# The second block's mixer: last gate projection emitted behind all else, recurrent heads two rounds later, small casts behind the gate products

## The chip, the cores and the metric

The kernel runs on one core of a Trainium2 chip. The metric is the device time of one execution in microseconds, lower is better. Engines are named as the profile names them: PE (TensorE, matmuls), PEld (its weight loads), DVE (VectorE), ACT (ScalarE), POOL (GpSimd), SP (SyncE, which here issues the loads of weights).

## The reference

A sequence of 256 tokens of 1024 features goes through two layers of a first block and then through one layer of a second. The change lies in the second block's mixer. There `proj = x @ w_in` is split into eight parts:

```python
q_a, k_a, v_a, f_a, q_r, f_r, i_r, g_r = jnp.split(proj, SPLIT_POINTS, axis=-1)
o_a = _fox_attention(heads(q_a, 8), heads(k_a, 8), heads(v_a, 8), logf_a)
o_a = _rms_norm_heads(o_a, fox_norm_g)
o_r = _hgrn2_chunked(heads(silu(q_r), 4), heads(k_r, 4), heads(i_r, 4), heads(logf_r, 4))
o_r = _rms_norm_heads(o_r, hgrn_norm_g) * silu(g_r)
mix = concatenate([o_a, o_r], axis=-1) @ w_o
x = _layer_norm(DEEPNORM_ALPHA * x + mix, ln_mix_g, ln_mix_b)
```

The attention has 8 heads of 64 features, causal, with a decay per head (`f_a`) added to the scores. The recurrent part has 4 heads of 128 features with a decay per feature (`f_r`). Both are normalised per head; the recurrent one is multiplied by the gate `silu(g_r)`. Then come the out projection `w_o`, a layer norm, and a feed-forward part with a convolution.

## The kernel before, in words

The whole model is one program. Weights stream from memory in blocks of 128 x 1024; each is split into a high part `wh` (a cast on ACT, L317) and a low part `wl` (a subtraction on DVE, L319), and there are five buffers for such pairs. A product is made of three matmuls (high x high, low x high, high x low), so that it keeps the precision of 32-bit floats. Each engine works through its own list of instructions strictly in order; a framework fixes these lists when the program is built, from the order in which the code emits the work, the engines' estimated times and the buffers. `issue_after(i)` adds a rule for one engine: what is emitted under it comes behind instruction `i` in that engine's list.

The mixer is `mix2` (L1165 to L1494). It emits its work from four generators that a loop of ticks calls in turn (L1460 to L1479). `main` (L1266) goes through the list `ORD`, `q0, va, q1, k2, q2, k3, q3, sg`: projections with the tokens as moving operand (L344 to L346, three matmuls of 128 x 256 a step, for q and k) or with the weights as moving operand (L373 to L375, 48 matmuls of 128 x 512 in all, for `va` and for the gate `sg`). `fox` (L1385) is the attention, head by head: scores (L1394, L1395), maximum and exponential, transposes (L1416), products with the values (L1426 to L1428). After four heads it normalises the group: multiplication by the reciprocal on DVE (L1439, into the tile `mix`), squares on POOL (L1442), sums on DVE (L1443), a reciprocal root in three small steps on ACT (L499 to L501) and four on POOL (L502 to L505), multiplication on DVE (L1448). Then `mixT` transposes the result on PE (L1356), ACT writes the high part `oh` (L1357) and DVE the low part `ol` (L1358).

`hgrn_a` (L1286) makes the decay tiles E of a recurrent head: matmuls with fixed patterns (L1298, L1299), exponentials on ACT (L1300), multiplications by k and q on DVE and POOL. `hgrn_b` (L1318) makes its score tile A level by level: matmuls (L1331), each put into A through a mask by DVE (L1332), a block between the two halves of the sequence (matmul L1336, copied into A by ACT, L1337), the product with the values (L1341 to L1343), copies into `mix` on DVE (L1346) and sums of squares on ACT (`jk`, L1348).

The out projection reads 1024 features in two halves: `out_half(0)` those of the attention, `out_half(1)` those of the recurrent heads. The latter need `hgrn_end` (L1360): eight products of `mix` with the reciprocal root `rrr` and the gate `sgr` (L1365, DVE), then `mixT`. The gate's silu (L1482) and the next exponentials need different tables on ACT, so a table load stands on either side of it. `def_begin` (L1097) casts the norm's gains and biases into the tiles of the layer norm, in twelve very small DVE operations (L1108, L1109).

Before, the gate projection waits in two ways: `main` yields until `fox` has been emitted whole, and on PE it comes behind the attention's last product:

```python
while fox in live:
    yield
with self.tc.issue_after(self.last_pv.ins):
    for _ in g:
        pass
```

Of the kernel before, what the change touches and what calls it, by code (L numbers as in the profile page):

```python
# [12 lines left out]
ALU = mybir.AluOpType  # L13
AX = mybir.AxisListType

P = 128
# [198 lines left out]
class K:  # L215
# [955 lines left out]
    def mix2(self, first):  # L1171
        nc = self.nc
# [55 lines left out]
        for tt in range(2):  # L1228
# [3 lines left out]
                                           op0=ALU.mult, op1=ALU.min)  # L1232
# [3 lines left out]
                                           op0=ALU.min, op1=ALU.subtract)  # L1236
# [6 lines left out]
        def projn(dst, fn=AF.Copy):  # L1243
            ps = [self.mm_ps() for _ in range(2)]
            yield from self.proj_n(ps)
            for tt in range(2):
                nc.scalar.activation(dst[:, tt], ps[tt], fn)
# [14 lines left out]
        sg = nat("sgr")  # L1262
# [3 lines left out]
        def main():  # L1266
            for d in ORD:
                if d == "va":
                    yield from projn(va)
                    made.add(d)  # L1270
                    continue
                if d == "sg":
                    g = projn(sg)
                    while fox in live:
                        yield
                    with self.tc.issue_after(self.last_pv.ins):
                        for _ in g:
                            pass
                    continue
                dst, t, sc = (fq if d[0] == "q" else fk), int(d[1]), (0.125 if d[0] == "q" else 1.0)  # L1280
                ps = self.mm_ps()[:, :T]
                yield from self.proj_t_steps(ps)
                nc.scalar.activation(dst[:, t], ps, AF.Copy, scale=sc)
                made.add(d)
# [3 lines left out]
        def hgrn_a():  # L1288
            for h in range(4):
                while h > len(done) + 1:  # L1290
                    yield
                E = [self.slot(f"E{tt}").rearrange("p (l t) -> p l t", l=8) for tt in range(2)]
                for tt in range(2):
                    for hf in range(2):
                        ps = self.mm_ps()
                        c = slice(hf * 512, (hf + 1) * 512)
                        hs = slice(h * P, (h + 1) * P)
                        nc.tensor.matmul(ps, lh[:, tt, hs], pat[tt][:, c], start=True, stop=False)  # L1298
                        nc.tensor.matmul(ps, ll[:, tt, hs], pat[tt][:, c], start=False, stop=True)  # L1299
                        nc.scalar.activation(E[tt][:, hf * 4:hf * 4 + 4], ps.rearrange("p (l t) -> p l t", l=4), AF.Exp)  # L1300
                    yield
                k3 = kT[:, h].rearrange("p (t c) -> p t c", t=2)
                q3 = qrT[:, h].rearrange("p (t c) -> p t c", t=2)
                nc.vector.tensor_tensor(out=E[0][:, 7], in0=E[0][:, 7], in1=k3[:, 0], op=ALU.mult)
                nc.vector.tensor_tensor(out=E[1][:, 7], in0=E[1][:, 7], in1=q3[:, 1], op=ALU.mult)
                for l, B in enumerate(LEVELS):
                    for o, src in ((0, k3), (1, q3)):
                        for tt in range(2):
                            v = E[tt][:, l].rearrange("p (n s b) -> p n s b", s=2, b=B)[:, :, o]
                            s = src[:, tt].rearrange("p (n s b) -> p n s b", s=2, b=B)[:, :, o]  # L1310
                            e = nc.gpsimd if (l * 4 + o * 2 + tt) % 8 == 0 else nc.vector
                            e.tensor_tensor(out=v, in0=v, in1=s, op=ALU.mult)
                hE[h] = E
                yield

        def hgrn_b():
            for h in range(4):
                while h not in hE:  # L1318
                    yield
                E = hE.pop(h)  # L1320
                k3 = kT[:, h].rearrange("p (t c) -> p t c", t=2)
                q3 = qrT[:, h].rearrange("p (t c) -> p t c", t=2)
                A = self.ap_.tile([P, 3, P], F32, tag="A", name="A", bufs=2)
                nc.gpsimd.memset(A, 0.0)
                for l2 in range(4):
                    ps = self.six_ps().rearrange("p (a b) -> p a b", a=2)
                    for li in range(2):
                        l = 2 * l2 + li
                        for tt in range(2):
                            a, b = (E[tt][:, l], E[tt][:, l]) if l < 7 else (k3[:, tt], q3[:, tt])  # L1330
                            nc.tensor.matmul(ps[:, li, tt * P:(tt + 1) * P], a, b, start=True, stop=True)  # L1331
                        nc.vector.copy_predicated(A[:, 0:2], msk[:, l].unsqueeze(1).to_broadcast([P, 2, P]),  # L1332
                                                  ps[:, li].rearrange("p (t c) -> p t c", t=2))
                    yield
                ps = self.aux_ps()
                nc.tensor.matmul(ps[:, :P], E[0][:, 7], E[1][:, 7], start=True, stop=True)  # L1336
                nc.scalar.activation(A[:, 2], ps[:, :P], AF.Copy)  # L1337
                yield
                ps = self.aux_ps()
                hs = slice(h * P, (h + 1) * P)  # L1340
                nc.tensor.matmul(ps[:, 0:P], A[:, 0], vr[:, 0, hs], start=True, stop=True)  # L1341
                nc.tensor.matmul(ps[:, P:2 * P], A[:, 2], vr[:, 0, hs], start=True, stop=False)
                nc.tensor.matmul(ps[:, P:2 * P], A[:, 1], vr[:, 1, hs], start=False, stop=True)  # L1343
                for tt in range(2):
                    o = mixn[tt][:, 512 + h * P:512 + (h + 1) * P]
                    nc.vector.tensor_copy(o, ps[:, tt * P:(tt + 1) * P])  # L1346
                    jk = self.tmp("jk", P, 2)
                    nc.scalar.activation(jk, ps[:, tt * P:(tt + 1) * P], AF.Square,  # L1348
                                         accum_out=ssr[:, tt * 4 + h:tt * 4 + h + 1])
                done.append(h)  # L1350
                yield

        def mixT(dst, src, gain):
            ps = self.aux_ps()
            for tt in range(2):
                nc.tensor.transpose(ps[:, tt * P:(tt + 1) * P], mixn[tt][:, src * P:(src + 1) * P], self.ident)  # L1356
            self.last_mix = nc.scalar.activation(OH(dst), ps[:, :T], AF.Copy, scale=gain)  # L1357
            nc.vector.scalar_tensor_tensor(out=OL(dst), in0=ps[:, :T], scalar=gain, in1=OH(dst).bitcast(F32),  # L1358
                                           op0=ALU.mult, op1=ALU.subtract)

        def hgrn_end(rr):
            for h in range(4):
                for tt in range(2):
                    o = mixn[tt][:, 512 + h * P:512 + (h + 1) * P]
                    nc.vector.scalar_tensor_tensor(out=o, in0=o, scalar=rr[:, tt * 4 + h:tt * 4 + h + 1],  # L1365
                                                   in1=sg[:, tt, h * P:(h + 1) * P], op0=ALU.mult, op1=ALU.mult)
            for t in range(4):
                mixT(4 + t, 4 + t, self.col("hgrn_g", t))

# [87 lines left out]
        OL = lambda t: ol[t // 4][:, (t % 4) * T:(t % 4 + 1) * T]  # L1457
        fox_bias()

        gens = [[main(), 14, 0, 0], [hgrn_a(), 10, 0, 0], [hgrn_b(), 10, 0, 0], [fox(), 10, 4, 0]]  # L1460
        fox_run = gens[3]
        live = [fox]
        tick = 0
        while gens:
            for g in list(gens):
                if tick < g[2]:
                    continue
                g[3] += g[1]
                while g[3] >= 10:
                    g[3] -= 10  # L1470
                    try:
                        next(g[0])
                    except StopIteration:
                        gens.remove(g)
                        if g is fox_run:
                            live.clear()
                        break
            tick += 1
        rr = self.rsqrt(ssr, 1.0 / P, self.tmp("rrr", 8, 1))  # L1479
        with self.tc.issue_after(self.last_mix.ins):  # L1480
            for tt in range(2):
# [3 lines left out]
        for _ in self.out_half(OH, OL, 0, None, ALPHA, six=True, tiles=range(6)):  # L1485
            pass
        self.ln_begin()
        self.def_begin("ln_mix_g", "ln_mix_b")
        for _ in self.out_half(OH, OL, 1, None, None, True, tiles=range(6)):
            pass  # L1490
        for _ in self.out_half(OH, OL, 0, None, ALPHA, True, tiles=range(6, 8), kn=8):
# [179 lines left out]
```

## Time and profile before

| | us |
|---|---|
| median of 3 runs | 1342.23 |
| lowest and highest | 1341.79 and 1344.1 |
| the profiled execution | 1342.08 |
| its span | 1340.3 |
| its mean granted clock of TensorE (1 is full) | 0.995 |
| busy in the span: PE, DVE, ACT, POOL | 1315.2, 996.5, 814.2, 218.5 |

The span runs from the first to the last instruction that the profiler recorded; the execution's time has some 1.8 us more around it. The mixer's stretch of which the following speaks begins at about 1022 us of the span and ends at about 1125, with the layer norm behind it. Busy times of PE are those of pipelined matmuls that overlap: one of 512 columns is shown 0.39 us long, while such matmuls start 0.23 us apart.

### The profile page before, as it was taken

To read this page: it belongs to the slowest core of one execution; us is meant where nothing else is said; L and a number is where in the kernel's file an instruction comes from. 1 tells how busy PE (TensorE), PEld (TensorE's weight loads), DVE (VectorE), ACT (ScalarE), POOL (GpSimd) and SP (SyncE) were. 2 spreads that over 40 slices of the span, in tenths; PEclk is the share of its full clock that TensorE was granted. 3 is DMA by queue.
4 is the path that set the end of the run, shared out by engine and by line. 5 is a ranking of instruction groups with operands and counts; after the bars stand their busy time and mean duration, and the time that the engine had idled before them with its cause. 6 is when DMAs were issued, how large, how long until landed. Compare 5 with 4: busy or idle time off the path is not lost.

```text
span 1340.3 us, 22596 instructions
## 1 busy us (share of the span) xinstructions
PE 1315.2 (98%) x8250; PEld 1169.3 (87%) x8250; DVE 996.5 (74%) x1863; ACT 814.2 (61%) x1501; POOL 218.5 (16%) x252
## 2 busy tenths in 40 slices
PE   9999999899999999999999999999999999999997
PEld 8888887898888888888889888888887888899987
DVE  7877677668776768776659768777887778798754
ACT  7655546756555446555458856555567546687642
POOL 2000140021000210001334440000033122232100
PEclk9999999899999999999999999999999999999999
DMA  8555555026555556555576336555555304365561
GB/s 309 187 189 189 188 202 179 1 95 204 189 188 177 197 171 198 189 189 186 187 235 203 115 128 209 187 190 188 186 185 192 126 32 155 114 221 177 198 208 47
DMA packets 64367, 231.49 MB, mean 173 GB/s; under 512 B 7352, under 2 KB 7488, under 8 KB 64256
## 3 DMA queue, kind: packets, MB, share of 16 engines
q1 hardware_dynamic: 61632, 221.41, 49.1%
q0 software_dynamic: 2480, 8.63, 1.9%
q8 instruction: 65, 1.06, 0.3%
q14 instruction: 46, 0.38, 0.1%
q10 hardware_dynamic: 144, 0.00, 0.0%
HBM read 228.96 MB, written 1.06 MB: 172 GB/s over the span
## 4 chain that ended last, share of the span: by engine, by line
PE 92%; DVE 3%; ACT 2%; issue 2%; DMA 1%; DVEq 0%; ACTq 0%
PE mm L340 26%; PE mm L338 14%; PE sc L340 7%; PE mm L344 5%; PE mm L345 5%; PE mm L346 5%; PE mm L375 4%; PE mm L373 4%; PE mm L374 4%; PE sc L338 4%; PE mm L337 3%; PE sc L337 1%; PE aux L686 1%; PE sc L344 1%; PE sc L345 1%
## 5 line engine op out<-in xcount | busy, mean ns | idle before, releaser
L319 DVE TENSOR_TENSOR wl<-raw,wh 128x1024 fp32r<-128x1024 f32 (+1 forms) x411 | 511.8, 1246 | 240.5 <-ACT wh L317 239.1
L317 ACT ACTIVATE wh<-raw 128x1024 fp32r<-128x1024 f32 (+1 forms) x419 | 441.1, 1055 | 407.0 <-issue 209.6
L340 PE MATMUL mm<-xs,wh 128*128 128x512 f32 x826 | 294.3, 396 | 0.0
L338 PE MATMUL mm<-xs,wl 128*128 128x256 f32 x944 | 243.9, 279 | 0.1
L340 PE MATMUL mm<-h,wh 128*128 128x512 f32 x672 | 238.0, 398 | 0.0
L338 PE MATMUL mm<-h,wl 128*128 128x256 f32 x704 | 191.5, 280 | 0.0
L338 PEld LDWEIGHTS mm<-xs,wl 128*128 128x128 f32 x944 | 177.9, 188 | 10.9 <-DVE wl L319 0.4
L340 PEld LDWEIGHTS mm<-xs,wh 128*128 128x128 f32 x826 | 154.6, 188 | 31.3
L340 PEld LDWEIGHTS mm<-h,wh 128*128 128x128 f32 x672 | 126.0, 188 | 29.2
L340 PE MATMUL sc<-xs,wh 128*128 128x512 f32 x406 | 144.8, 396 | 0.0
L338 PEld LDWEIGHTS mm<-h,wl 128*128 128x128 f32 x704 | 132.9, 189 | 3.1
L476 POOL TENSOR_TENSOR sq<-xt 128x256 f32<-128x256 f32 x40 | 36.0, 903 | 538.7 <-DVE xt L606 351.6
L338 PE MATMUL sc<-xs,wl 128*128 128x256 f32 x464 | 119.9, 279 | 0.0
L345 PE MATMUL mm<-xs,wh 128*128 128x256 f32 x384 | 109.5, 286 | 2.1 <-DVE xs L1094 2.1
L344 PE MATMUL mm<-xs,wh 128*128 128x256 f32 x384 | 109.9, 288 | 0.4 <-ACT wh L317 0.4
L346 PE MATMUL mm<-xs,wl 128*128 128x256 f32 x384 | 109.3, 286 | 0.0
L338 PEld LDWEIGHTS sc<-xs,wl 128*128 128x128 f32 x464 | 87.5, 189 | 5.2
L340 PEld LDWEIGHTS sc<-xs,wh 128*128 128x128 f32 x406 | 76.1, 188 | 15.6
L345 PEld LDWEIGHTS mm<-xs,wh 128*128 128x128 f32 x384 | 74.0, 193 | 2.4 <-DVE xs L1094 2.3
L344 PEld LDWEIGHTS mm<-xs,wh 128*128 128x128 f32 x384 | 73.6, 193 | 2.3 <-issue 1.5
L346 PEld LDWEIGHTS mm<-xs,wl 128*128 128x128 f32 x384 | 74.1, 193 | 0.9 <-issue 0.8
L373 PE MATMUL mm<-wh,xs 128*128 128x512 f32 x144 | 57.1, 396 | 0.0
(398 smaller groups left out, 2578.0 us busy)
## 6 DMA issues: line engine op xcount, KB each, us to landing
raw<-wst SPq DMA_DIRECT2D x417, 512.0 KB, 3.3
m1b<-m1bias POOLq DMA_DIRECT2D x8, 512.0 KB, 5.0
xt<-xT SPq DMA_DIRECT2D x4, 256.0 KB, 6.0
patf<-m2pat POOLq DMA_DIRECT2D x2, 512.0 KB, 8.2
kb<-scr POOLq DMA_DIRECT2D x2, 512.0 KB, 4.7
out<-x2n SPq DMA_DIRECT2D x4, 256.0 KB, 2.0
raw<-wst SPq DMA_DIRECT2D x2, 256.0 KB, 4.3
m0tab<-m0tab POOLq DMA_DIRECT2D x1, 512.0 KB, 3.9
```

Source lines behind the costliest of these rows:

```text
L317: self.nc.scalar.activation(wh[:, c], r[:, c], AF.Copy)
L319: e.tensor_tensor(out=wl[:, c], in0=r[:, c], in1=wh[:, c].bitcast(F32), op=ALU.subtract)
L337: mm(ps, wh, x2, start=True, stop=False)
L338: mm(ps[:, :T], wl, x2[:, :T], start=False, stop=False, skip_group_check=True)
L340: mm(ps, wh, x2, start=False, stop=last)
L344: mm(ps, wh, xh, start=first, stop=False)
L345: mm(ps, wh, xl, start=False, stop=False)
L346: mm(ps, wl, xh, start=False, stop=last)
L373: mm(ps, xh, wh, start=first, stop=False)
L374: mm(ps, xh, wl, start=False, stop=False)
L375: mm(ps, xl, wh, start=False, stop=last)
L476: nc.gpsimd.tensor_tensor(out=sq, in0=self.x(j), in1=self.x(j), op=ALU.mult)
```

## The change

There are three edits in `mix2`. The gate projection is taken out of `main` and emitted after the loop of ticks, with no rule on what it must follow. `hgrn_a` and `hgrn_b` begin at tick 2 rather than 0. And `def_begin` is emitted under `issue_after` of the last gate product, so that its casts come behind these on DVE. Lines behind L1273 have numbers that are lower by five or six in the changed kernel.

```diff
                 if d == "sg":
-                    g = projn(sg)
-                    while fox in live:
-                        yield
-                    with self.tc.issue_after(self.last_pv.ins):
-                        for _ in g:
-                            pass
                     continue
...
-                    nc.vector.scalar_tensor_tensor(out=o, in0=o, scalar=rr[:, tt * 4 + h:tt * 4 + h + 1],
-                                                   in1=sg[:, tt, h * P:(h + 1) * P], op0=ALU.mult, op1=ALU.mult)
+                    self.last_o = nc.vector.scalar_tensor_tensor(
+                        out=o, in0=o, scalar=rr[:, tt * 4 + h:tt * 4 + h + 1],
+                        in1=sg[:, tt, h * P:(h + 1) * P], op0=ALU.mult, op1=ALU.mult)
...
-        gens = [[main(), 14, 0, 0], [hgrn_a(), 10, 0, 0], [hgrn_b(), 10, 0, 0], [fox(), 10, 4, 0]]
-        fox_run = gens[3]
-        live = [fox]
+        gens = [[main(), 14, 0, 0], [hgrn_a(), 10, 2, 0], [hgrn_b(), 10, 2, 0], [fox(), 10, 4, 0]]
...
-                        if g is fox_run:
-                            live.clear()
                         break
             tick += 1
+        for _ in projn(sg):
+            pass
         rr = self.rsqrt(ssr, 1.0 / P, self.tmp("rrr", 8, 1))
...
-        self.def_begin("ln_mix_g", "ln_mix_b")
+        with self.tc.issue_after(self.last_o.ins):
+            self.def_begin("ln_mix_g", "ln_mix_b")
```

The lists of the engines move more than these lines say. In the rows that follow, mm, sc and aux are accumulators in PSUM, and a number behind a tile's name is that of its buffer. The first place is PE at the attention's last products with the values (L1426 to L1428 before, L1421 to L1423 now), where `mix` is the tile that `fox` normalises. Before:

```order
L1426 MATMUL mm<-va,pT 128x64
L1427 MATMUL mm<-va,pT 128x64
L1428 MATMUL mm<-va,pT 128x64
L373 MATMUL mm<-wh,xs_10438 128x512
L374 MATMUL mm<-wl,xs_10438 128x512
L375 MATMUL mm<-wh,xs_10438 128x512
L373 MATMUL mm<-wh,xs_10438 128x512
L374 MATMUL mm<-wl,xs_10438 128x512
L375 MATMUL mm<-wh,xs_10438 128x512
```

Now:

```order
L1421 MATMUL mm<-va,pT 128x64
L1422 MATMUL mm<-va,pT 128x64
L1423 MATMUL mm<-va,pT 128x64
L344 MATMUL mm<-oh_10976,wh 128x256
L345 MATMUL mm<-ol_10978,wh 128x256
L346 MATMUL mm<-oh_10976,wl 128x256
L344 MATMUL mm<-oh_10976,wh 128x256
L345 MATMUL mm<-ol_10978,wh 128x256
L346 MATMUL mm<-oh_10976,wl 128x256
L1350 MATMUL aux<-ident,mix_10967 128x128 x2
L1350 MATMUL aux<-ident,mix_10968 128x128 x2
```

Before, the 48 matmuls of the gate projection follow the last of these products. Now that projection stands ahead of it, and behind the product there are six matmuls of `out_half(0)` and then the transposes of the normalised `mix` (L1356 before, L1350 now).

The second place is PE ahead of the recurrent half of the out projection. Before, at the first transposes of the gated `mix`:

```order
L346 MATMUL mm<-oh_10976,wl 128x256
L344 MATMUL mm<-oh_10976,wh 128x256
L345 MATMUL mm<-ol_10978,wh 128x256
L346 MATMUL mm<-oh_10976,wl 128x256
L1356 MATMUL aux<-ident,mix_10967 128x128
L344 MATMUL mm<-oh_10976,wh 128x256
L345 MATMUL mm<-ol_10978,wh 128x256
L1356 MATMUL aux<-ident,mix_10967 128x128
L346 MATMUL mm<-oh_10976,wl 128x256
L344 MATMUL mm<-oh_10976,wh 128x256
L345 MATMUL mm<-ol_10978,wh 128x256
L346 MATMUL mm<-oh_10976,wl 128x256
```

Now, from the product of the last recurrent head (L1336, L1337) on:

```order
L1337 MATMUL aux<-vr,A 128x128
L346 MATMUL mm<-oh_10976,wl 128x256
L344 MATMUL sc<-oh_10976,wh 128x256
L345 MATMUL sc<-ol_10978,wh 128x256
L346 MATMUL sc<-oh_10976,wl 128x256
L345 MATMUL sc<-ol_10978,wh 128x256
L346 MATMUL sc<-oh_10976,wl 128x256
L344 MATMUL sc<-oh_10976,wh 128x256
L345 MATMUL sc<-ol_10978,wh 128x256
L346 MATMUL sc<-oh_10976,wl 128x256
L1350 MATMUL aux<-ident,mix_10967 128x128
L1350 MATMUL aux<-ident,mix_10968 128x128
```

Before, the last head's product lay inside the gate projection, and the gated transposes were spread among matmuls of `out_half(0)`. Now nine matmuls of `out_half(0)` lie between the product and the gated transposes.

The third place is ACT around the gate's silu (L1482 before, L1475 now). Before:

```order
L1357 ACTIVATE oh_10976<-aux,cols 128x256 x2
L1247 ACTIVATE sgr<-mm 128x512
L317 ACTIVATE wh<-raw 128x1024
L1247 ACTIVATE sgr<-mm 128x512
L1482 ACT_TABLE_LOAD
L1482 ACTIVATE sgr<-sgr 128x512 x2
L564 ACT_TABLE_LOAD
L317 ACTIVATE wh<-raw 128x1024 x2
L1357 ACTIVATE oh_10977<-aux,cols 128x256 x2
```

Now:

```order
L1351 ACTIVATE oh_10976<-aux,cols 128x256 x2
L1475 ACT_TABLE_LOAD
L1475 ACTIVATE sgr<-sgr 128x512 x2
L564 ACT_TABLE_LOAD
L1331 ACTIVATE A<-aux 128x128
L317 ACTIVATE wh<-raw 128x1024 x2
L1342 ACTIVATE jk,ssr<-aux 128x128
L317 ACTIVATE wh<-raw 128x1024
L1342 ACTIVATE jk,ssr<-aux 128x128
L499 ACTIVATE nw_11926<-ssr,eps 128x8
L500 ACTIVATE nw_11925<-nw_11926 128x8
L501 ACTIVATE nw_11925<-nw_11925 128x8
```

Now the copy of the last head's block into A (L1331) stands behind both table loads; before, the copy of that head came ahead of the whole piece shown. The evictions `sgr` of the gate projection have moved up, and the sums of squares `jk` of the last head with the root behind them have moved down.

## Rows read from the trace of the kernel before

**Rows 1.** The page of the kernel before, part 1: engine, busy us (share of span), instructions.

```profile
PE 1315.2 (98%) x8250; PEld 1169.3 (87%) x8250; DVE 996.5 (74%) x1863; ACT 814.2 (61%) x1501; POOL 218.5 (16%) x252
```

**Rows 2.** Windows (us): length, busy time and instructions by engine, granted clock, DMA share, GB/s.

```profile
1020.00:1030.00 10.00, 8.67 (x53) 7.18 (x52) 8.87 (x15) 8.84 (x18) 4.39 (x3) 1.00 0.69 215
...
1080.00:1090.00 10.00, 8.99 (x71) 8.01 (x70) 8.63 (x39) 5.06 (x21) 1.99 (x6) 1.00 0.00 0
...
1090.00:1100.00 10.00, 9.22 (x64) 7.97 (x63) 5.08 (x13) 3.69 (x12) 1.19 (x2) 1.00 0.01 2
```

**Rows 3.** Timeline, PE: start us, us, line, operation, tiles, count [idle before <-releaser].

```profile
1028.87 0.50 PE L1298 MATMUL mm<-patr,lh 128*128 128x512 f32 x1 [0.96 <-ACT E L1300]
...
1089.37 0.71 PE L1331 MATMUL mm<-E 128*128 128x128 f32 x4 [1.00 <-DVE A L1332]
...
1119.73 0.41 PE L1356 MATMUL aux<-ident,mix 128*128 128x128 f32 x2 [0.84 <-DVE dh L1108]
```

**Rows 4.** Timeline, PE: gate projection's first and last matmul, out_half(1)'s first ones.

```profile
1097.29 0.48 PE L373 MATMUL mm<-wh,xs 128*128 128x512 f32 x1
...
1108.98 0.40 PE L375 MATMUL mm<-wh,xs 128*128 128x512 f32 x1
...
1118.25 0.64 PE L344 MATMUL mm<-oh,wh 128*128 128x256 f32 x4
```

**Rows 5.** Timeline, DVE, same columns, 1097 to 1116.

```profile
1097.51 0.76 DVE L1439 TENSOR_TENSOR mix<-mm,frd 128x256 f32<-128x256 f32 x2 [2.91 <-PE mm L1428]
...
1099.24 0.42 DVE L1443 TENSOR_REDUCE fss<-sq 128x4 f32<-128x256 f32 x1 [0.15 <-POOL sq L1442]
...
1104.61 1.23 DVE L319 TENSOR_TENSOR wl<-raw,wh 128x1024 fp32r<-128x1024 f32 x1
...
1113.08 2.19 DVE L1365 SCALAR_TENSOR_TENSOR mix<-mix,rrr,sgr 128x128 f32<-128x128 f32 x8 [1.27 <-ACT sgr L1482]
...
1115.18 1.08 DVE L1608 SCALAR_TENSOR_TENSOR xt<-xt,mm 128x256 f32<-128x256 f32 x3
```

**Rows 6.** Timeline, POOL, two tails of the attention.

```profile
1087.65 0.20 POOL L502 TENSOR_TENSOR nw<-nw 128x8 f32<-128x8 f32 x1 [2.40 <-ACT nw L501]
...
1088.51 0.20 POOL L505 TENSOR_TENSOR frr<-nw,nw 128x8 f32<-128x8 f32 x1
...
1098.02 1.19 POOL L1442 TENSOR_TENSOR sq<-mix 128x256 f32<-128x256 f32 x2 [9.31 <-DVE mix L1439]
```

**Rows 7.** Timeline, ACT, same columns, 1086 to 1117.

```profile
1086.80 0.29 ACT L499 ACTIVATE nw<-fss,eps 128x8 f32<-128x8 f32 x1
...
1087.36 0.21 ACT L501 ACTIVATE nw<-nw 128x8 f32<-128x8 f32 x1
...
1103.12 0.28 ACT L1348 ACTIVATE jk<-aux 128x128 f32<-128x128 f32 x1 [0.96 <-DVE mix L1346]
...
1108.27 0.84 ACT L1357 ACTIVATE oh<-aux,cols 128x256 fp32r<-128x256 f32 x2 [0.97 <-PE aux L1356]
...
1111.05 1.28 ACT L1482 ACT_TABLE_LOAD   x1
...
1112.35 1.15 ACT L1482 ACTIVATE sgr<-sgr 128x512 f32<-128x512 f32 x2
...
1113.52 1.28 ACT L564 ACT_TABLE_LOAD   x1
...
1114.81 2.21 ACT L317 ACTIVATE wh<-raw 128x1024 fp32r<-128x1024 f32 x2
```

**Rows 8.** Windows of 5 us behind two longer waits of PE.

```profile
235.00:240.00 5.00, 3.04 (x18) 2.56 (x15) 4.26 (x7) 3.63 (x12) 0.00 (x0) 0.77 0.00 0
...
1160.00:1165.00 5.00, 5.00 (x34) 5.00 (x34) 4.58 (x12) 3.48 (x7) 0.00 (x0) 0.73 0.61 211
```

**Rows 9.** Timeline, PE: the two waits ahead of those windows.

```profile
237.29 1.17 PE L905 MATMUL mm<-kv,pT 128*128 128x64 f32 x6 [1.96 <-ACT pT L688]
...
1158.24 0.38 PE L345 MATMUL mm<-xs,wh 128*128 128x256 f32 x1 [2.08 <-DVE xs L1094]
```

## The prediction

> **What bounds the kernel now.** The page comes first: PE is busy for 98% of the span [rows 1], so the time is PE's work plus what PE waits. Then the windows over the second block's mixer, from the end of the last recurrent projection to the out projection: in most slices of 10 us PE is full, and three show idle time, 1.33, 1.01 and 0.78 us [rows 2]. The timeline of PE names the waits there: 0.96 us for ACT's exponential E, 1.00 us for a DVE mask, and 0.84 us at the second half of the out projection [rows 3]. A wait costs more from start to start than its idle time, because the pipelined matmuls around it lose their overlap: laid against the usual distances (0.12 us a 256-column matmul, 0.23 us a 512-column one), what PE loses between 1024.9 and 1118.25 comes to about 5.5 us, and 1.0 us more at the last of these waits. I take that as the sum of both shortfalls: 3.1 us idle by the windows, and some 2.4 us of lost overlap at about eight interruptions.
>
> The work between the same points is not changed by the edit. So the question is only which waits PE meets in the new order, and PE, as each engine, takes its rows strictly in that order.
>
> What the last gate projection does now: it is 48 matmuls from 1097.29 to 1108.98 [rows 4], and begins right behind the last product of the attention. The attention's own tail runs beneath it: multiplication by the reciprocal on DVE at 1097.51, squares on POOL at 1098.02, sums on DVE to 1099.66, and the result stands as oh at 1108.27 [rows 5 to 7]. So does the recurrent tail, whose products with the gate come at 1113.08 [rows 5]. That is 12 us of cover, followed by 9 us of out_half(0) up to 1118.25 [rows 4].
>
> **The change, part by part.**
>
> *Start of the stage.* Behind q0, PE now goes straight into the va projection, with the transposes of kr and the first E matmuls between its matmuls. The wait of 0.96 us and its neighbours go; one comes back, since an E matmul needs a PSUM buffer that ACT frees only behind a weight cast (1.06 us: 2.21 for two [rows 7]). I keep 1.0 us of waits here.
>
> *Middle.* The gate projection now sits ahead of head 3's last masks and of three attention heads, and fills the holes at 1080 to 1100 [rows 2]. It begins when a DVE mask has given a PSUM buffer back, and DVE has about as much work queued as PE there: I keep 1.5 us. Of 5.5 us lost before, 2.5 stay: **-3.0** (bounds -5.5 and 0).
>
> *Attention's tail.* Now only six matmuls of 0.12 us stand on PE between the last attention product and the four transposes that need the normalised mix, and those six wait for mix themselves. The chain in between is priced by its rows: from the start of the first multiplication to the end of the second sum 2.15 us (1097.51 to 1099.66 [rows 5]), three small ACT steps 0.77 (1086.80 to 1087.57), four POOL steps 1.06 (1087.65 to 1088.71), two multiplications 0.76 like those at 1097.51, and a hand-over of 0.2: 4.9 us [rows 5 to 7]. Less 0.7 us of work: **+4.2**. Then oh must be evicted (0.41 us each, 0.84 for two [rows 7]) before the matmuls behind it: **+0.4**. Bounds of both 4.0 and 6.5: the low end without hand-overs, the high end with one or two weight casts (2.21 us for two [rows 7]) ahead of ACT's steps.
>
> *Head 3 behind the table loads.* On ACT the copy of head 3's A tile now stands behind oh, a table load of 1.28, two silus (1.15) and a second load of 1.28 [rows 7]: 3.7 us. It holds up head 3's last product. PE has about 2.6 us of out_half(0) in that time, counted from the matmul that feeds the copy, and the mask-free part of the product: **+0.9** (0 to 2). The Trainium skill, page "ScalarE: Activation LUTs", section "What ACT_TABLE_LOAD costs", puts a switch at about 2.66 us, 1.28 for the load and the rest for a drain. By that the sum would be an estimated 2.7 us larger. The trace disagrees: silu starts at 1112.35, 0.02 us behind the end of the load, so the row of 1.28 is the whole price.
>
> *Gate chain.* This is the largest term. Behind head 3's product PE has nine matmuls left (1.1 us), and then transposes of the gated tiles. Between them lie, one after the other: DVE's copy of mix and one update of xt (0.3 and 0.33), a weight subtraction wl (1.2), two updates (0.7; 1.08 for three), another wl (1.2), the second copy (0.3), ACT's sum of squares (0.5), the three ACT steps (0.77), the four POOL steps (1.06), and two of the eight gate products (0.55 of 2.19) [rows 5 to 7]. The two wl are in the chain because DVE's order puts them ahead of the second copy. Sum 6.9, with hand-overs 7.0 us; less 1.1 of work **+5.9**, and 0.65 for oh's eviction: **+6.55** (4.5 to 8; the low end is without one wl and with quick hand-overs). Before, the same chain ended beneath the gate projection.
>
> *Casts.* The twelve small casts now follow the gate products, in the gaps between ol's; three weight subtractions and the updates are done by then too. The wait of 0.84 us at 1119.73 [rows 3], which really came from ol, late behind wl (1.22 at 1104.61, like the ones around 1118 [rows 5]), goes: **-1.0** (0 to -1.2).
>
> *Clock.* Two waits on PE of about two microseconds were each followed by a lower granted clock: 1.96 us at 237.29, with 0.77 in 235:240, and 2.08 us at 1158.24, with 0.73 in 1160:1165 [rows 8, 9]. So part of such a slice ran at the lower of the two levels, 1.2 against 2.4 GHz, and 0.27 of 5 us, 1.35 us, were lost. The two new waits of 4 and 6 us are longer than these. Behind the first, the wait for the table loads hides most of it; behind the second, out_half(1) is on the path: **+1.4** (0 to 3).
>
> Nothing else moves in price: POOL and SP have the same rows, and every weight is loaded once. Behind out_half(1) DVE sets the pace to about 1141, by rows in the same order as before and waiting for out_half(1)'s first tile, so a late start there is passed on whole.
>
> Sum: -3.0 + 4.6 + 0.9 + 6.55 - 1.0 + 1.4 = **+9.45 us**. The profiled execution took 1342.08 (span 1340.3), 0.15 below the median of 1342.23; so 1351.5, and I say **1351**.
>
> **The rivals.**
> *The holes are filled and the tails stay hidden* (faster). The gate projection fills 1080 to 1100, and the chains end beneath out_half(0): -5.5 - 1.0 gives 1335.6, or 1337 with a wait kept. It decides by whether the rsqrt and gate chains end within the work left behind their last product on PE. Against it: that work is 0.7 and 1.1 us, the chains are 4.9 and 7.0. Chance 0.06.
> *Taken back later* (no change). What out_half(1) loses, the stage behind it regains, because DVE did its weight subtractions during the wait. For it: DVE has no idle time from 1126 to 1141. Against it: five of those subtractions stand behind out_half(1)'s first tile, before and now. About 1342. Chance 0.07.
> *Dear table loads* (slower still). A drain holds the copy of A, and with it head 3, the gate chain and the out projection: 1351.5 + 2.7 = 1354. That is what the Trainium skill's rule from above would make of it, under the same page and section; the rows don't bear it out. Chance 0.08.
> *Late weights* (slower still). The new order bunches casts behind the gate projection, and subtractions hold up masks and copies at both chains: two more wl each, some 5 us, 1356. Chance 0.1.
>
> **How the numbers follow.** The forecast has 0.69, of which a third is without the clock's fall or with other terms at their low bounds (down to 1346). The range, 1345 to 1357, takes in the forecast's bounds and both slower rivals, and leaves out the rivals that are not slower and the outer ends. About 0.2% (2.7 us) is what a measurement can tell: slower by more 0.87, within 0.07, faster 0.06.
>
> **What would show it.** In the profile after: no wait of 0.96 us before va; PE with two idle stretches, of about 4 us ahead of the second group of attention transposes (released by DVE's mix, in a chain by POOL's frr) and about 6 us ahead of the gated transposes (released by DVE's gate product); a wait of about 1 us on ACT's copy A between them; a granted clock under 1.00 behind the longer one; out_half(1) some 9 us later than 1118.25, and the same distance from there to the end. Wrong if PE idles less than 5 us in these places together, or if the distance from out_half(1) to the end has shrunk by several microseconds.

## The result, and the profile after

The changed kernel takes 1352.65 us (median of 4 runs, 1351.39 to 1353.36); the kernel before, measured beside it, 1343.16 (4 runs, 1341.79 to 1344.64). The ratio is 1.0071 [1.0059, 1.0083]: slower by 9.5 us, where some 2.7 can be told from no change. The profiled execution took 1352.05, its span is 1350.3 against 1340.3. The profiled executions of all kernels reach the last wait that they share ahead of the mixer's stage (PE for DVE's xs, L1094) between 996.2 and 1000.0 us of their spans, although the program ahead of it is the same. So traces are compared within the stage: at most from that wait to the row of L1065, the sums of the layer norm.

First the page of the changed kernel, the span and part 1:

```profile
span 1350.3 us, 22602 instructions
...
PE 1317.7 (98%) x8250; PEld 1170.9 (87%) x8250; DVE 997.6 (74%) x1863; ACT 813.6 (60%) x1501; POOL 214.6 (16%) x252
```

PE executes the same 8250 matmuls [rows 1] and still counts 98%, yet it is busy 2.5 us longer: the same work at a lower clock (the four matmuls that took 0.64 us at the start of out_half(1) [rows 4] take 1.22 below). A busy share can't show 10 us of waiting here; the list of PE's waits does (what was waited for: us in total, times, longest):

```profile
PE aux L1350 <- DVE mix L1359: 5.5, 1, 5.5
...
PE aux L1350 <- DVE mix L1443: 2.8, 1, 2.8
...
PE mm L344 <- DVE mix L1434: 0.9, 1, 0.9
...
PE mm L344 <- ACT oh L1351: 0.4, 1, 0.4
```

All four are new. None of the waits of [rows 3] is left: neither the 0.96 for E, nor the 1.00 for the mask A, nor the 0.84 at out_half(1). (The change shortens the code, so lines read 5 to 7 lower than before.) The windows of the changed kernel, first slices of 10 us, then of 2 us:

```profile
1020.00:1030.00 10.00, 10.00 (x59) 8.73 (x58) 9.23 (x9) 7.76 (x12) 5.03 (x4) 1.00 0.71 227
1080.00:1090.00 10.00, 9.80 (x71) 8.85 (x72) 8.79 (x42) 4.34 (x18) 2.40 (x7) 1.00 0.00 0
1090.00:1100.00 10.00, 10.00 (x53) 8.42 (x53) 5.64 (x9) 4.46 (x6) 0.00 (x0) 1.00 0.14 39
...
1110.00:1120.00 10.00, 7.16 (x42) 6.72 (x43) 2.83 (x9) 6.59 (x12) 0.81 (x4) 0.66 0.01 2
1120.00:1130.00 10.00, 4.47 (x22) 3.71 (x21) 8.67 (x31) 4.67 (x13) 0.80 (x4) 0.71 0.48 158
...
1112.00:1114.00 2.00, 1.16 (x5) 0.72 (x5) 0.82 (x3) 0.56 (x2) 0.00 (x0) 0.50 0.00 0
1114.00:1116.00 2.00, 2.00 (x9) 2.00 (x10) 0.82 (x2) 1.97 (x3) 0.00 (x0) 0.50 0.00 0
...
1128.00:1130.00 2.00, 2.00 (x10) 2.00 (x11) 1.92 (x16) 0.67 (x2) 0.00 (x0) 0.50 0.18 72
```

The three slices that had holes [rows 2] are full, so the change does what it sets out to do. It opens two larger holes behind them, and the granted clock is at its lower level, 0.50 of full speed, behind each. PE's timeline goes through them, from the last wait ahead of the stage:

```profile
997.43 0.73 PE L375 MATMUL mm<-wh,xs 128*128 128x512 f32 x2 [0.40 <-DVE xs L1094]
...
1107.46 0.39 PE L1423 MATMUL mm<-va,pT 128*128 128x64 f32 x2
1108.79 0.36 PE L344 MATMUL mm<-oh,wh 128*128 128x256 f32 x1 [0.94 <-DVE mix L1434]
...
1109.46 0.28 PE L346 MATMUL mm<-oh,wl 128*128 128x256 f32 x1
1112.49 1.12 PE L1350 MATMUL aux<-ident,mix 128*128 128x128 f32 x4 [2.76 <-DVE mix L1443]
1113.96 1.22 PE L344 MATMUL mm<-oh,wh 128*128 128x256 f32 x4 [0.35 <-ACT oh L1351]
...
1119.23 0.39 PE L1336 MATMUL aux<-vr,A 128*128 128x128 f32 x2
1119.45 0.39 PE L1337 MATMUL aux<-vr,A 128*128 128x128 f32 x2
...
1120.63 0.28 PE L346 MATMUL sc<-oh,wl 128*128 128x256 f32 x1
1126.41 1.27 PE L1350 MATMUL aux<-ident,mix 128*128 128x128 f32 x4 [5.50 <-DVE mix L1359]
1127.71 1.22 PE L344 MATMUL mm<-oh,wh 128*128 128x256 f32 x4
...
1147.88 0.39 PE L345 MATMUL mm<-dl,wh 128*128 128x258 f32 x1 [1.38 <-DVE dl L1116]
...
1151.57 1.10 PE L1065 MATMUL aux<-lacc,ones 128*128 128x512 f32 x2 [0.26 <-DVE wgb L1136]
```

In the kernel before, the first of these rows reads:

```profile
997.74 0.73 PE L375 MATMUL mm<-wh,xs 128*128 128x512 f32 x2 [0.42 <-DVE xs L1094]
```

The row at 1107.46 is the last attention product, the one at 1119.45 head 3's last. Behind each PE has its few matmuls and then nothing but transposes of a tile that DVE has yet to write. out_half(1) begins at 1127.71, 9.46 later than before [rows 4]. What PE waits for stands on DVE, here from 1112 to 1128:

```profile
1112.01 0.76 DVE L1443 TENSOR_TENSOR mix<-mix,frr 128x256 f32<-128x256 f32 x2 [1.98 <-POOL frr L505]
...
1119.88 0.29 DVE L1340 COPY mix<-aux 128x128 f32<-128x128 f32 x1
...
1120.41 1.22 DVE L319 TENSOR_TENSOR wl<-raw,wh 128x1024 fp32r<-128x1024 f32 x1
...
1122.21 1.22 DVE L319 TENSOR_TENSOR wl<-raw,wh 128x1024 fp32r<-128x1024 f32 x1
1123.35 0.28 DVE L1340 COPY mix<-aux 128x128 f32<-128x128 f32 x1
...
1126.01 2.19 DVE L1359 SCALAR_TENSOR_TENSOR mix<-mix,rrr,sgr 128x128 f32<-128x128 f32 x8 [1.24 <-POOL rrr L505]
```

The two copies of head 3's result stand 3.47 us apart, with two weight subtractions between them, and the gate products follow the second copy by 2.66: the chain that the prediction listed, in its order. On ACT, in the same stretch:

```profile
1113.43 0.84 ACT L1351 ACTIVATE oh<-aux,cols 128x256 fp32r<-128x256 f32 x2 [2.59 <-PE aux L1350]
1114.29 1.28 ACT L1475 ACT_TABLE_LOAD   x1
1115.58 1.15 ACT L1475 ACTIVATE sgr<-sgr 128x512 f32<-128x512 f32 x2
1116.75 1.28 ACT L564 ACT_TABLE_LOAD   x1
1118.04 0.28 ACT L1331 ACTIVATE A<-aux 128x128 f32<-128x128 f32 x1
```

Head 3's A is ready at 1118.32, behind oh, load, silu and load, as forecast. But PE comes to its product (L1336) only at 1119.23 and waits for nothing.

### The profile page after: what moved, and what is told of

Its sections match the earlier page's. It is cut to its first block, busy times and chain, and to the rows that moved or that the text cites. A ratio compares the mean times of both kernels' runs of the same rounds, so it can differ in the third digit from the quotient of the medians.

```text
span 1350.3 us, 22602 instructions
## 1 busy us (share of the span) xinstructions
PE 1317.7 (98%) x8250; PEld 1170.9 (87%) x8250; DVE 997.6 (74%) x1863; ACT 813.6 (60%) x1501; POOL 214.6 (16%) x252
## 3 DMA queue, kind: packets, MB, share of 16 engines
q8 instruction: 65, 1.06, 0.3%
HBM read 228.96 MB, written 1.06 MB: 170 GB/s over the span
## 4 chain that ended last, share of the span: by engine, by line
PE 92%; DVE 4%; ACT 3%; issue 1%; POOL 0%; DVEq 0%; ACTq 0%; POOLq 0%
PE mm L340 26%; PE mm L338 14%; PE sc L340 7%; PE mm L344 5%; PE mm L345 5%; PE mm L346 5%; PE sc L338 4%; PE mm L375 4%; PE mm L373 4%; PE mm L374 4%; PE mm L337 3%; PE sc L337 1%; PE sc L344 1%; PE sc L346 1%; PE sc L345 1%
```

## The experiments

Each kernel was measured against the kernel before on the same chip, in three rounds (five for the two that are named so). The theory is the prediction's: each edit moves work from behind a product to a place ahead of it, and the chain of small steps behind that product is then bare.

**The gate projection alone.** The changed kernel, with the recurrent heads back at tick 0 and the casts where they were:

```diff
-        gens = [[main(), 14, 0, 0], [hgrn_a(), 10, 2, 0], [hgrn_b(), 10, 2, 0], [fox(), 10, 4, 0]]
+        gens = [[main(), 14, 0, 0], [hgrn_a(), 10, 0, 0], [hgrn_b(), 10, 0, 0], [fox(), 10, 4, 0]]
...
-        with self.tc.issue_after(self.last_o.ins):
-            self.def_begin("ln_mix_g", "ln_mix_b")
+        self.def_begin("ln_mix_g", "ln_mix_b")
```

> Only the gate projection is emitted behind the loop; recurrent heads start at tick 0 and the casts stand as before. Theory (each move uncovers one chain): the holes at 1080 to 1100 go (-3), the attention's tail is uncovered (+4.6 and a lower clock behind it, +1.5), the last head's product still comes early, so the gate chain stays mostly under out_half(0) (+1): about +4 us against before, 1347, and PE waits about 4 us for the attention's mix but under 2 us for the gated tiles. Rival (the projection's move alone makes the loss, by both chains): +9 us or more, 1352, with a wait of over 4 us at the gated tiles too.

Measured 1348.09 us against 1343.91, ratio 1.0029 [1.0016, 1.0042]: +4.2. PE's timeline of this run has the wait of the attention's tail, and none at the first gated transposes; only the one at their next pair, 0.84 before [rows 3], is longer:

```profile
1114.39 0.77 PE L1350 MATMUL aux<-ident,mix 128*128 128x128 f32 x4 [2.93 <-DVE mix L1443]
...
1124.29 0.41 PE L1350 MATMUL aux<-ident,mix 128*128 128x128 f32 x2 [1.46 <-DVE dh L1108]
```

**The later start alone.** The kernel before, with one line changed:

```diff
-        gens = [[main(), 14, 0, 0], [hgrn_a(), 10, 0, 0], [hgrn_b(), 10, 0, 0], [fox(), 10, 4, 0]]
+        gens = [[main(), 14, 0, 0], [hgrn_a(), 10, 2, 0], [hgrn_b(), 10, 2, 0], [fox(), 10, 4, 0]]
```

> Only the recurrent heads start two ticks later; the gate projection still follows the attention's last product. Theory (each move uncovers one chain): the wait ahead of va goes (-1.3), the attention's tail stays under the gate projection, but the last head's product comes with only 16 matmuls (1.9 us) of out_half(0) left, so the gate chain of 7 us is uncovered (+5.7, clock +1.4, end -1): about +5 us, 1348, with a wait of about 5 us ahead of the gated transposes and none at the attention's. Rival (the later start is a gain, the loss is all the projection's): -1 to -2 us, 1341, no wait over 1.5 us there.

Measured 1349.76, ratio 1.0045 [1.003, 1.006]: +5.9. The wait of 0.96 at the start is gone, the middle has waits of 1.01, 0.85 and 0.58, and the big one stands where the theory has it, though shorter than the 5 us expected:

```profile
1123.72 1.12 PE L1356 MATMUL aux<-ident,mix 128*128 128x128 f32 x4 [3.62 <-DVE mix L1365]
```

So each of the two edits bares one chain and not the other. +4.2 and +5.9 make 10.1, against 9.5 for both together: within the intervals they add. The traces are finer: from the last wait ahead of the stage to the row of L1065 the two cost 4.7 and 7.1 us, and both together 10.3. So each alone also costs something that the two together do not, 1.5 us in all; the wait of 1.46 above is a part of it.

**The later start and the casts; the casts alone.** To the line above the third edit is added, and then that edit is made by itself:

```diff
-        self.def_begin("ln_mix_g", "ln_mix_b")
+        with self.tc.issue_after(self.last_o.ins):
+            self.def_begin("ln_mix_g", "ln_mix_b")
```

> Later start and casts behind the gate products, gate projection as before. Theory: as with the later start alone within 0.7 us, about 1348, since the casts cost DVE 1 us in a stretch where it waits. Rival (casts ahead of ol hold it up): 1 us or more faster than the later start alone.

> Only the casts are put behind the gate products. Theory: PE's order is that of before, ol was late by a weight subtraction and not by casts, so nothing to gain: -0.5 to +0.3 us, 1343. Rival (the wait of 0.84 us released by a cast's row was the casts'): -1 us, 1342.

Measured 1349.29, ratio 1.0043 [1.0028, 1.0058], with the same wait of 3.62, and for the casts alone 1343.27, ratio 0.9993 [0.9984, 1.0003], with the wait of 0.83 at out_half(1) still there. The third edit is worth nothing that can be measured, in either company, and the casts were not what made that wait.

**The weight subtractions out of the gate chain.** The changed kernel, with the weights of out_half(0)'s last part prepared behind the last eviction:

```diff
+        self.behind = [self.last_ol, self.last_mix]
         for _ in self.out_half(OH, OL, 0, None, ALPHA, six=True, tiles=range(6)):
             pass
+        self.behind = None
```

> The changed kernel, but the three weight casts and subtractions that lay between the last head's product and the gate products come behind the last oh and ol of the gated tiles. Theory (the gate chain of 7 us holds two weight subtractions): the wait ahead of the gated transposes falls from 5.5 us by 2.4 to 3.3 us; two of the three subtractions then fall into DVE's idle time during out_half(1), one into the stage that DVE bounds, +1.2: net -1 to -2.5 us against the changed kernel, about 1351. Rival (what sets the chain is the small steps of ACT and POOL and the hand-overs): that wait stays over 4.5 us and the time within 0.7 us of 1352.6.

Measured 1355.46 against 1343.48, ratio 1.0085 [1.007, 1.01], where the changed kernel has 1.0071 [1.0059, 1.0083]. The gain of 1 to 2.5 us did not come. PE's timeline says why:

```profile
1126.09 1.28 PE L1350 MATMUL aux<-ident,mix 128*128 128x128 f32 x4 [2.91 <-DVE mix L1359]
1135.43 0.35 PE L344 MATMUL mm<-oh,wh 128*128 128x256 f32 x1 [0.51 <-ACT wh L317]
1148.73 0.39 PE L345 MATMUL mm<-dl,wh 128*128 128x258 f32 x1 [2.87 <-DVE dl L1116]
1155.03 1.10 PE L1065 MATMUL aux<-lacc,ones 128*128 128x512 f32 x2 [0.67 <-DVE lacc L1037]
```

The wait at the gated transposes falls from 5.50 to 2.91, as it should: two subtractions of 1.22 were in the chain. But the three subtractions are still to be done, and behind out_half(1) DVE has no room: the wait for dl is 2.87 instead of 1.38. From the attention's transposes to the row of L1065 it is 40.24 us here (1114.79 to 1155.03) and 39.08 in the changed kernel (1112.49 to 1151.57): 2.6 won, 3.8 lost. The subtractions that lengthened the wait were done there at less than they cost later. Where they went matters, too: the expectation had two of the three fall into DVE's idle time during out_half(1), but the edit puts all of them behind the last ol (1131.64), and DVE stands idle for 2.04 us ahead of the gate products and for 1.60 ahead of that ol. A place in those gaps was not tried.

**Useless matmuls in both waits.** The changed kernel, with PE kept busy, to see what the lower clock costs: 7 matmuls ahead of the attention's second transposes and 9 ahead of the gated ones, then 7 and 15 (that one beside the two last experiments below). Each makes two rows in the trace.

```diff
+            for _ in range({2: 7, 4: 9}.get(dst, 0)):
+                with self.tc.issue_after(self.last_pv.ins):
+                    nc.tensor.matmul(ps[:, :T], self.ident, kT[:, 0], start=True, stop=True)
```

> The changed kernel with matmuls that compute nothing of use on PE in the two long waits (7 of 256 columns behind the attention's last product, 9 ahead of the gated transposes; their results are overwritten). Theory (the lower clock behind the waits costs 3 to 4 us of the 9.5): the granted clock stays at 1.00 there, matmuls of out_half stand 0.12 us apart behind both waits instead of 0.21, and the time is 3 to 4 us shorter than the changed kernel's, about 1349. Rival (a lower clock is hidden by the waits for ACT and DVE): the clock stays up and the time does not move by more than 1 us, 1352.

> As the run with matmuls of no use in the waits, with 15 instead of 9 of them in the second wait, so that PE is busy up to about 0.5 us ahead of the gated transposes. Theory (the lower clock behind the second wait is on the path, behind the first it was hidden by the table loads): out_half(1)'s matmuls stand 0.12 us apart, and the time is 1 to 2 us below the run with 9, about 1351. Rival (DVE's stage behind takes it back): the clock stays up, the time is within 0.5 us of that run.

With 7 and 9: 1352.24 against 1343.48, ratio 1.0063 [1.0048, 1.0078], which can't be told from the changed kernel: the 3 to 4 us of the theory did not come. With 7 and 15: 1351.39 against 1343.5, ratio 1.0057 [1.0043, 1.0071], 0.85 under the run with 9, between what the theory and the rival had (it ran on another chip, on which the kernel before takes the same time). The windows of the first of them show where the filling was too short, the clock being 1.00 behind the first wait and low behind the second:

```profile
1110.00:1120.00 10.00, 8.68 (x63) 7.84 (x62) 5.29 (x13) 7.89 (x12) 0.56 (x3) 1.00 0.01 2
1120.00:1130.00 10.00, 6.80 (x30) 5.69 (x29) 6.53 (x26) 2.67 (x10) 0.81 (x4) 0.70 0.51 157
```

and the windows of the second run have it at 1.00 in both:

```profile
1110.00:1120.00 10.00, 8.69 (x59) 7.75 (x59) 3.40 (x9) 5.22 (x9) 1.99 (x6) 1.00 0.01 2
1120.00:1130.00 10.00, 9.36 (x50) 7.69 (x49) 7.62 (x19) 5.46 (x14) 0.80 (x4) 1.00 0.49 158
```

PE's timeline of that second run:

```profile
1114.75 0.77 PE L1353 MATMUL aux<-ident,mix 128*128 128x128 f32 x4 [0.86 <-DVE mix L1446]
...
1120.82 0.39 PE L1336 MATMUL aux<-vr,A 128*128 128x128 f32 x2
1121.05 0.39 PE L1337 MATMUL aux<-vr,A 128*128 128x128 f32 x2
1121.27 6.64 PE L1351 MATMUL aux<-kTr,ident 128*128 128x256 f32 x30
1128.49 1.11 PE L1353 MATMUL aux<-ident,mix 128*128 128x128 f32 x4 [0.58 <-DVE mix L1362]
...
1152.59 1.10 PE L1065 MATMUL aux<-lacc,ones 128*128 128x512 f32 x2 [0.26 <-DVE wgb L1136]
```

PE idles 0.58 us ahead of the gated transposes instead of 5.50, and the kernel is hardly faster. From the attention's transposes to the row of L1065 it takes 37.84 us (1114.75 to 1152.59) against 39.08: 1.24 less, 0.66 of them up to L1337 (6.30 against 6.96) and 1.06 behind the gated transposes, while the gate chain between (7.44 against 6.96) is longer by 0.48.

The edit changes more than the filling, though. In both runs the nine matmuls of out_half(0) that stood behind L1337 now stand ahead of L1336, so PE passes L1337 0.66 earlier although it has done 1.1 us more of work; and DVE does three weight subtractions instead of two ahead of its second copy, which is why the chain is longer. So 1.24 is what the filled kernel wins in this stretch, and not a clean price of the clock. With the chain at its old length it would be 1.7; and the two filled runs, whose order up to the gated transposes is the same, differ by 1.64 from there to the row of L1065 (25.74 with 9, 24.10 with 15). An estimate from these numbers: the lower clock costs between 1.2 and 2.3 us of the 9.5 (0.66 and 1.64 at the upper end). The rest is the chains' own length: while they run, PE's speed and its idleness change little.

**A faster pace for the later heads.** The kernel before, with the recurrent heads at tick 2 and 14 instead of 10 tenths of a step per tick; then with half of the gate projection's matmuls let in front, in the middle's holes, and the rest left behind the last product (`npv` counts the heads whose product has been emitted):

```diff
-        gens = [[main(), 14, 0, 0], [hgrn_a(), 10, 0, 0], [hgrn_b(), 10, 0, 0], [fox(), 10, 4, 0]]
+        gens = [[main(), 14, 0, 0], [hgrn_a(), 14, 2, 0], [hgrn_b(), 14, 2, 0], [fox(), 10, 4, 0]]
```

> The kernel before, with recurrent heads that start two ticks later but get 14 tenths of a turn per tick instead of 10, so that the last head's product comes ahead of the gate projection. Theory (the later start is good for the wait ahead of va, and bad only by the late last head): the waits of 0.36 and 0.96 us go, both tails lie under the gate projection: -1.3 to -2.5 us, 1341.5. Rival (the heads crowd DVE while the attention runs, and the wait comes back as one for masks): 0 to +3 us, 1344 to 1347.

```diff
                     g = projn(sg)
+                    while self.npv < 6:
+                        yield
+                    with self.tc.issue_after(self.last_pv.ins):
+                        for _ in range(2):
+                            next(g)
                     while fox in live:
                         yield
```

> As the kernel with faster recurrent heads, and half of the gate projection (24 matmuls) may run from the sixth head's product on, the other half follows the attention's last product. Theory: the first half fills holes between the last heads, the second half (5.5 us) with 20 matmuls of out_half(0) still covers the attention's tail of 4.9 us: 1 to 2 us below the kernel with faster heads alone, 1340. Rival (nothing was left to fill, and the second half is too short a cover): the same as that kernel or up to 3 us above.

The pace alone: 1344.42, ratio 1.0012 [1.0, 1.0023]. The heads end in time, so the tail stays covered; the stalls at the start are gone, but in the middle PE now meets waits of 1.02 for E and 0.97 for ol among others. Nothing is won; in the trace, the stage up to the row of L1065 is 2.8 us longer than before. With half of the projection in front: 1351.58, ratio 1.0053 [1.0036, 1.007]. Two waits come at out_half(1), where none was due:

```profile
1125.82 1.22 PE L344 MATMUL mm<-oh,wh 128*128 128x256 f32 x4 [2.44 <-ACT oh L1363]
...
1128.75 0.69 PE L1362 MATMUL aux<-ident,mix 128*128 128x128 f32 x2 [1.71 <-DVE ol L1364]
```

Half of the projection still covers the attention's tail, whose transposes wait for nothing, but not the gate's: the gate products on DVE begin at 1120.72, and ol comes behind six updates and three weight subtractions at 1128.22.

**Everything later, the cover kept.** Five rounds each: the kernel before with the attention moved as well, from tick 4 to 6, so that the heads keep their distance to it; and the same with one weight preparation of out_half(0) moved behind an eviction, so that the ol ahead of out_half(1) is not late.

```diff
-        gens = [[main(), 14, 0, 0], [hgrn_a(), 10, 0, 0], [hgrn_b(), 10, 0, 0], [fox(), 10, 4, 0]]
+        gens = [[main(), 14, 0, 0], [hgrn_a(), 10, 2, 0], [hgrn_b(), 10, 2, 0], [fox(), 10, 6, 0]]
```

> The kernel before, with the recurrent heads and the attention both two ticks later (2, 2 and 6), so that the head start of the recurrent heads over the attention stays as it was. Theory (the later start is a gain ahead of va, and its loss was only that the last head's product fell behind the gate projection): PE's order at both tails is that of before, the waits of 0.36 and 0.96 us go: -1 to -2 us, 1341.5 to 1342.5. Rival (the wait only moves to the next place where E is needed, as it did with the faster heads): no difference, 1343 to 1344.

```diff
-        for _ in self.out_half(OH, OL, 0, None, ALPHA, six=True, tiles=range(6)):
+        for _ in self.out_half(OH, OL, 0, None, ALPHA, six=True, tiles=range(2)):
+            pass
+        self.behind = [self.ols[5]]
+        for _ in self.out_half(OH, OL, 0, None, ALPHA, six=True, tiles=range(2, 6)):
             pass
+        self.behind = None
```

> As the kernel with everything later, and one weight subtraction that stood ahead of the first ol of the gated tiles is put behind the second ol. Theory (that ol was late by the subtraction, not by the casts): the wait of 0.84 us at the second half of the out projection falls under 0.3 us and 0.7 to 1 us is gained on the kernel with everything later, 1341. Rival (the time is given back, since DVE sets the pace behind it): the wait goes but the time stays.

All later: 1343.48 against 1343.5, ratio 0.9996 [0.9988, 1.0005]. The start's stalls are replaced by one of 0.73 (for E, at 1037.64), the rest is as before. With the preparation moved: 1342.15, ratio 0.9991 [0.9982, 1.0]. The wait of 0.84 [rows 3] is gone; in this run's PE timeline the same transposes follow with none:

```profile
1120.53 0.64 PE L344 MATMUL mm<-oh,wh 128*128 128x256 f32 x4
1121.01 0.38 PE L1357 MATMUL aux<-ident,mix 128*128 128x128 f32 x2
```

So a weight subtraction had made that ol late. The median is the lowest of the study, 1.3 us under the kernel before, but the interval reaches 1.0. In the traces the stage up to the row of L1065 is 0.6 us shorter than before, and 0.4 shorter than in the run with everything later, whose wait here was 0.82. So a real gain is not shown, and part of the wait is given back, as the rival had it.

## Why the prediction was right, and where its terms were off

The forecast was 1351 from 1342.23, a rise of 8.8 (its sum: 9.45). Measured against the runs beside it the rise is 9.5, and the time, 1352.65, lies inside the range. Most of the signs that the prediction named are there: no wait of 0.96 ahead of the va projection; two idle stretches of 3.7 and 5.5 us, where about 4 and 6 were forecast, released by DVE's mix through POOL's frr and by DVE's gate product; a lower clock behind the longer one; out_half(1) 9.46 us later, and from there to the end of the span 222.6 us against 222.1. One is not: between the two there is no wait for ACT's copy A.

The two profiles allow an account by place. From the last common wait ahead of the stage (997.74 before, 997.43 after) to the first matmul of out_half(1) it is 120.51 us before and 130.28 after, with the same work, so PE loses 5.5 + 9.77 = 15.3 us there instead of 5.5.

| term | forecast | measured | from |
|---|---|---|---|
| stalls at the start and in the middle | -3.0 | -3.8 | by difference: 15.3 less the 13.6 of the next rows is 1.7, where 5.5 were lost before |
| attention's tail and its oh | +4.6 | +5.2 | 1107.66 to 1113.96 is 6.3, less 1.1 of matmuls |
| head 3 behind the table loads | +0.9 | 0 | no wait at 1119.23 |
| clock behind the first wait | hidden | +1.7 | 1113.96 to 1119.6, against the usual distances |
| gate chain and its oh | +6.55 | +6.7 | 1119.6 to 1127.71 is 8.1, less 1.4 of matmuls |
| casts' wait and clock at out_half(1) | -1.0 + 1.4 | +0.5 | to the wait for dl: 19.65 before (1118.25 to 1137.90), 20.17 after (1127.71 to 1147.88) |
| sum | +9.45 | +10.3 | less 0.3 ahead of the stage: the spans' 10.0 |

*The stalls.* The gate projection filled the middle's holes better than the 1.5 us of waits that were kept for it: the three slices together idle for 0.20 us.

*The chains* were right in place, in order and nearly in size. They could be priced from durations in the trace of before, because the steps were the same and only their cover went. That each edit bares its own chain is shown by the first two experiments. That the chain sets the time, and not what PE does meanwhile, is shown by the last filling run, in which PE is busy through nearly all of the second wait.

*Table loads and clock: the mis-sized step.* The prediction had PE wait 0.9 us for A, and let this wait hide the clock's loss behind the first of the two long waits. It went the other way round. The clock's loss there, 1.7 us, is the larger, and it hid the table loads: A was ready 0.9 us before PE asked. Had PE been at full speed in the same order, it would have come 1.7 earlier, at 1117.5, and waited 0.8 for A at 1118.32. That is worked out and was not tested: in the filling runs, in which PE was at full speed, nine more matmuls stand ahead of the product, and in the last of them A is ready at 1120.35 and PE comes at 1120.82. They do bear out the 1.7, since the product came 0.66 earlier with 1.1 us more of work ahead of it. Of two delays in parallel only the longer counts, and the prediction took the wrong one for the longer: the term was 0.8 too small. The attention's tail was 0.6 too small, and the stalls, 0.8 too large in what they left, made up for part of both. That the total came so close is in this part luck: without it the sum would have been 1.7 short instead of 0.85.

*The casts.* "Which really came from ol, late behind wl" was right, and so the casts' edit was nothing: made alone it leaves the wait, and a moved subtraction takes it away. (The one ahead of that ol is at 1117.97; in the row at 1104.61 that the prediction quotes it takes 1.23 us, not 1.22.) In the changed kernel the wait is gone because out_half(1) comes so late that the subtractions are done, and not because of the casts: with the later start alone, where the casts stand as before, there is no wait at this place either.

*The dear table loads* are out: silu starts at 1115.58, 0.01 behind the load's end (1114.29 + 1.28), and the copy of A 0.01 behind the second one. The 2.66 us a switch of the Trainium skill ("ScalarE: Activation LUTs", "What ACT_TABLE_LOAD costs") are not seen here either.

*Taken back later* is out too: the distance to the wait for dl has grown by 0.5, and the run without the subtractions shows the reason. The stage behind is DVE's, and what DVE is not given during the wait it must do there.

What stays open: whether the holes at the start and in the middle could be filled without touching the cover. Four runs tried it and none gained more than its interval; in the three that moved only the order of the generators or of the gate projection, other waits took the place of those removed.

## What to carry to other kernels

A stretch of independent matmuls behind the last product of a stage can be the cover of the chain that turns this product into the next operand. Before such work is moved forward into holes, write down that chain step by step, with every instruction that stands between its steps on the engines it crosses, and compare its length with the matmuls that are left behind the product: here 0.7 and 1.1 us were left for chains of 5 and 7, and holes of 3.8 were paid for with 13.6. And work of another engine that stands in such a chain is not saved by taking it out: here 2.6 us were won in the wait and 3.8 lost behind it, where that engine had no room.

## What was not expected of the hardware

The granted clock fell already behind the first of the new waits: it is 0.50 from 1112 to 1116, behind waits of 0.94 and 2.76 us with 0.9 us of matmuls between them. Matmuls of 256 columns then start 0.21 us apart instead of 0.12, until about 1117.3; behind the wait of 5.50 it is the same from 1127.71 to 1130.9. Waits that stay at 0.86, 0.46 and 0.58 left it at 1.00 in the last filling run, and so did those of about 1 us before the change [rows 2, 3]. Yet the price of both falls is only some 1.2 to 2.3 us, by the estimate above. That work on PE which computes nothing made the kernel no slower, and if anything slightly faster, was the clearest sign that the bound had left PE, while the page went on showing it busy for 98% of the span.
